# Branch gates, branch products and attention's queries and keys computed transposed, in a two-block mixer network on one core

## The chip, the cores and the metric

The kernel runs on 1 core of one Trainium2 chip. The metric is the device time of one execution in microseconds, as the median of several runs.

## The reference, cut to what matters

One sequence of 256 tokens, 1024 channels, float32. A first block of two layers (mixer, then a dense or an expert feed-forward part, then a gated side input) is followed by a second block of two layers with another mixer. The parts that the change touches are in the two mixers:

```
# first block's mixer, once per layer; u is the normalised input, (256, 1024)
rq, rk, rv, rg, gqkv, gz, ga, gb, mg_ret, mg_gdn = split(u @ w_in)
q = rotary(rq, pos); k = rotary(rk, pos)           # 4 heads of 128
# rotary: x1, x2 = halves of a head; [x1 * cos - x2 * sin, x2 * cos + x1 * sin]
y_ret = (norm(retention(q, k, rv)) * silu(rg)) @ w_br_ret
y_gdn = (norm(gated_delta_rule(gqkv ...)) * silu(gz)) @ w_br_gdn
merged = sigmoid(mg_ret) * y_ret + sigmoid(mg_gdn) * y_gdn
h = h + merged @ w_out

# second block's mixer, once per layer
uf, dq, dk, dv, gq, gk, gv, gr, glr = split(u @ w_in_2)
pool = windowed means of uf, mixed by a small matrix
diff = for each of 4 heads: (softmax(q1 k1') - lam * softmax(q2 k2')) @ dv    # q, k from dq, dk
gla  = gated linear attention of gq, gk, gv, with gate gr and decay from glr
h = h + concat(pool, diff, gla) @ w_out
```

## The kernel before

Everything lives in SBUF for the whole run except weights, which stream from HBM in tiles of 128 by 1024 values (`raw`). Matmuls run on tiles of the program's type fp32r. To keep accuracy, each product is made of three matmuls: every weight tile is split into a high part `whi` by ACT (L248) and a rest `wlo` by DVE (L249), every activation into `uh` and `ul` in the same way (L251 on ACT, L252 on DVE), and the three products high by high, low by high and high by low go into the same PSUM bank.

There are two forms of a product. `linear` (matmuls at L196 to L198) holds 128 tokens of the activation still and streams 512 columns of weights past them; its result is natural, tokens on partitions. `blocks_t` (L240 to L242) holds a 128 by 128 block of weights still and streams the 256 tokens past it; its result is transposed, channels on partitions, two blocks of 128 channels in one bank. `blocks_t` wants the weights in another order in HBM, which the host prepares. Whatever is computed in natural form and is wanted with channels on partitions goes through `split_t` (L264: a transpose on TensorE against the identity `c_ident`, into a `pt` bank, then L251 and L252).

The program keeps PSUM in two pools of four banks: `mm` for the products, `pt` for everything else.

In the first block's mixer the natural form made: the rotary queries and keys `qr`, `kr` (four wide DVE operations per 128 tokens, with one position per partition), the gates `mgr` and `mgg` (ACT, sigmoid with the token's norm `R` as a per-partition factor, L646), the two branch products (L743 and the line ahead of it multiply by the gate and add). Retention transposes each head of `qr` and `kr` (L702: 4 transposes a head, 16 a layer) and copies them out (`qkt`, L705) before its scores (L707, L708) and outputs (L713 to L715). The merged result `mgr` is transposed (L264, 16 a layer) for `w_out`.

In the second block's mixer `dq` and `dk` are made in natural form and copied out of PSUM by ACT with the factor `R` (L1055); after the gated linear attention (`gla`; its last matmuls are L1147 and L1149, its output `glo`, L1152 and L1153, then eight squares on ACT, L1157, a reciprocal root in 12 small DVE operations, L145 to L153, and eight products `gy`, L1165, transposed at L264) they are transposed a head at a time (L1189, 16 a layer) and copied to `qt` and `kz` (L1193 to L1196). `kz` keeps the two half-heads in separate zero-padded blocks. The scores are L1206.

The order on each engine is decided when the program is built, by a list scheduler with its own estimates: it starts instructions by priority, the chains (retention, delta rule, gla, softmax) ahead of projections, and projections fill TensorE's waits as far as weights and free PSUM banks allow. After that every engine has its list of instructions, in that order. A bank of `mm` can be filled again only after ACT or DVE has emptied it.

`row_of` (L295 to L300) turns the per-token factor `R` into a row `Rrow`, equal on all partitions, by two float32 matmuls (L297) and a DVE copy (L299). Before, the first block's mixer calls it once per layer, and the second block's mixer doesn't.

## Time and profile before

| | |
|---|---|
| median of 3 runs | 1987.58 us (1984.10 to 1988.67) |
| the profiled execution | 1985.24 us, its span 1983.5 us |
| TensorE busy | 1947.6 us, 98% of the span |
| VectorE busy | 1459.9 us, 74% |
| ScalarE busy | 1186.6 us, 60% |
| mean granted TensorE clock | 0.996 of full speed |

Times in rows are microseconds from the start of the span. Matmuls overlap in TensorE's pipeline, so a matmul's own duration says less than the distance from its start to the next one's start. A row that ends in `xN` is N instructions of one kind that follow each other; a bracket at a row's end is idle time of the engine just ahead of it, and what ended that.

### The profile page before, as it was taken

To read this page: it belongs to the slowest core of one execution; us is meant where nothing else is said; L and a number is where in the kernel's file an instruction comes from. 1 tells how busy PE (TensorE), PEld (TensorE's weight loads), DVE (VectorE), ACT (ScalarE), POOL (GpSimd) and SP (SyncE) were. 2 spreads that over 40 slices of the span, in tenths; PEclk is the share of its full clock that TensorE was granted. 3 is DMA by queue.
4 is the path that set the end of the run, shared out by engine and by line. 5 is a ranking of instruction groups with operands and counts; after the bars stand their busy time and mean duration, and the time that the engine had idled before them with its cause. 6 is when DMAs were issued, how large, how long until landed. Compare 5 with 4: busy or idle time off the path is not lost. (4 is left out here: it accounts for less than half of the span.)

```text
span 1983.5 us, 30564 instructions
## 1 busy us (share of the span) xinstructions
PE 1947.6 (98%) x11386; PEld 1665.2 (84%) x11386; DVE 1459.9 (74%) x2569; ACT 1186.6 (60%) x1885; POOL 14.3 (1%) x29
## 2 busy tenths in 40 slices
PE   7999999999999999999999999998999999999998
PEld 7888887999889878877888888786879898879896
DVE  7986756666479877666998888897877555776565
ACT  7862454544478743445877777776765454565453
POOL 0000000000000000001000000000000000000000
PEclk9999999999999999999999999999999999999999
DMA  9553445565565553456798989994735665635653
GB/s 241 150 169 113 133 161 175 179 186 187 191 176 157 157 156 105 151 193 217 253 350 300 354 298 355 325 355 159 227 107 159 191 184 179 182 96 176 189 188 106
DMA packets 244926, 393.27 MB, mean 198 GB/s; under 512 B 23297, under 2 KB 100001, under 8 KB 244769
## 3 DMA queue, kind: packets, MB, share of 16 engines
q1 hardware_dynamic: 235344, 389.14, 61.2%
q10 hardware_dynamic: 9424, 2.10, 0.5%
q8 instruction: 91, 1.49, 0.3%
q14 instruction: 67, 0.54, 0.1%
HBM read 389.35 MB, written 1.84 MB: 197 GB/s over the span
## 5 line engine op out<-in xcount | busy, mean ns | idle before, releaser
L249 DVE TENSOR_TENSOR wlo<-raw,whi 128x1024 fp32r<-128x1024 f32 (+3 forms) x748 | 878.8, 1184 | 380.6 <-ACT whi L248 373.1
L248 ACT ACTIVATE whi<-raw 128x1024 fp32r<-128x1024 f32 (+3 forms) x748 | 766.1, 1027 | 586.9 <-PE mm L198 354.5
L196 PE MATMUL mm<-whi,uh 128*128 128x512 f32 (+3 forms) x1312 | 504.8, 385 | 2.0 <-ACT uh L251 1.5
L197 PE MATMUL mm<-wlo,uh 128*128 128x512 f32 (+3 forms) x1312 | 504.0, 385 | 1.0 <-DVE wlo L249 0.5
L198 PE MATMUL mm<-whi,ul 128*128 128x512 f32 (+3 forms) x1312 | 503.5, 386 | 0.8 <-DVE ul L252 0.6
L197 PEld LDWEIGHTS mm<-wlo,uh 128*128 128x128 f32 x1312 | 247.0, 188 | 51.9 <-DVE wlo L249 6.9
L196 PEld LDWEIGHTS mm<-whi,uh 128*128 128x128 f32 x1312 | 247.1, 188 | 48.4 <-ACT uh L251 4.6
L198 PEld LDWEIGHTS mm<-whi,ul 128*128 128x128 f32 x1312 | 246.3, 188 | 46.2 <-DVE ul L252 2.2
L240 PE MATMUL mm<-uh,whi 128*128 128x256 f32 x864 | 242.3, 281 | 0.7 <-ACT uh L251 0.6
L242 PE MATMUL mm<-uh,wlo 128*128 128x256 f32 x864 | 242.0, 280 | 0.0
L241 PE MATMUL mm<-ul,whi 128*128 128x256 f32 x864 | 242.0, 280 | 0.0
L240 PEld LDWEIGHTS mm<-uh,whi 128*128 128x128 f32 x864 | 162.7, 188 | 1.8 <-ACT uh L251 1.1
L241 PEld LDWEIGHTS mm<-ul,whi 128*128 128x128 f32 x864 | 162.6, 188 | 0.2
L242 PEld LDWEIGHTS mm<-uh,wlo 128*128 128x128 f32 x864 | 162.7, 188 | 0.0
L198 PE MATMUL mm<-whi,hl 128*128 128x512 f32 x344 | 136.4, 397 | 0.0
L197 PE MATMUL mm<-wlo,hh 128*128 128x512 f32 x344 | 135.7, 394 | 0.0
L196 PE MATMUL mm<-whi,hh 128*128 128x512 f32 x344 | 134.5, 391 | 0.0
L224 PE MATMUL mm<-uh,wlo 128*128 128x256 f32 x384 | 109.9, 286 | 0.0
L222 PE MATMUL mm<-uh,whi 128*128 128x256 f32 x384 | 109.6, 285 | 0.0
L223 PE MATMUL mm<-ul,whi 128*128 128x256 f32 x384 | 109.6, 285 | 0.0
L251 ACT ACTIVATE uh<-pt,cols 128x256 fp32r<-128x256 f32 x152 | 65.1, 472 | 20.8 <-PE pt L264 7.4
L197 PEld LDWEIGHTS mm<-wlo,hh 128*128 128x128 f32 x344 | 64.6, 188 | 15.2
(419 smaller groups left out, 2423.1 us busy)
## 6 DMA issues: line engine op xcount, KB each, us to landing
raw<-in_w_in_dram SPq DMA_DIRECT2D x176, 512.0 KB, 3.7
raw<-in_w_mlp_dram SPq DMA_DIRECT2D x128, 512.0 KB, 3.7
raw<-in_exp_w_down_dram SPq DMA_DIRECT2D x80, 512.0 KB, 6.7
raw<-in_exp_w_gate_dram SPq DMA_DIRECT2D x64, 512.0 KB, 5.6
raw<-in_exp_w_up_dram SPq DMA_DIRECT2D x64, 512.0 KB, 6.1
raw<-in_w_out_dram SPq DMA_DIRECT2D x32, 512.0 KB, 3.6
raw<-in_exp_w_gate_dram SPq DMA_DIRECT2D x32, 384.0 KB, 4.6
raw<-in_exp_w_up_dram SPq DMA_DIRECT2D x32, 384.0 KB, 4.2
```

The source lines that it names most:

```text
L196: nc.tensor.matmul(o, uh[:, u0 + k, tk], hi, start=first and k == 0, stop=False)
L197: nc.tensor.matmul(o, uh[:, u0 + k, tk], lo, start=False, stop=False)
L198: nc.tensor.matmul(o, ul[:, u0 + k, tk], hi, start=False, stop=last and k == kt - 1)
L222: nc.tensor.matmul(o[:, m], hi[:, k], uh[:, k, :], start=k == 0, stop=False)
L223: nc.tensor.matmul(o[:, m], hi[:, k], ul[:, k, :], start=False, stop=False)
L224: nc.tensor.matmul(o[:, m], lo[:, k], uh[:, k, :], start=False, stop=k == 7)
L240: nc.tensor.matmul(o[:, i], hi[:, k], uh[:, k, :], start=k == 0, stop=False)
L241: nc.tensor.matmul(o[:, i], hi[:, k], ul[:, k, :], start=False, stop=False)
L242: nc.tensor.matmul(o[:, i], lo[:, k], uh[:, k, :], start=False, stop=k == 7)
L248: nc.scalar.activation(hi, src, AF.Copy)
L249: nc.vector.tensor_sub(lo, src, hi.bitcast(F32))
L251: nc.scalar.activation(hi, src, AF.Copy, scale=col)
```

## The change

All in the two mixers; the layout of six weights on the host goes with it.

- First block's mixer: rotary queries and keys come out of `blocks_t` (weights `w_rqk`, with the two halves of the heads on separate blocks), so that DVE makes two products with cosine and sine rows and four short sums and differences for each pair of blocks, and `qkt` is written directly in the form that the scores want. `cosR` and `sinR`, the rows with the token's factor in them, are made once a layer by POOL. Retention's 16 transposes and four copies a layer go.
- The gates `mgr`, `mgg` come out of `blocks_t` (`w_mg`): DVE multiplies by `Rrow`, ACT takes the sigmoid. The branch products come out of `blocks_t` too; the last of them is split for `w_out` right where it is merged, and the 16 transposes of `mgr` a layer go.
- Second block's mixer: `dq` and `dk` come out of `blocks_t` (`w_dqk`). DVE multiplies them by `Rrow` straight into `qt` and `kz`; the 16 transposes a layer and their copies go. `Rrow` is made here by a new call of `row_of`.

Counted in the two programs, 1152 matmuls of 128 by 512 become 2304 of 128 by 256; 96 transposes go, and 4 small float32 matmuls (two calls of `row_of`) are new. Bytes from HBM and the number of weight splits stay.

```diff
-            def rotary(name, dst):
-                o = [s.mm(), s.mm()]
-                s.linear(u, W, 0, 8, OFF[name], 512, o)
...
+            def rotary(n):
+                for pr in range(2):
+                    o = s.mm().rearrange("p (m t) -> p m t", t=T)
+                    s.blocks_t(u, a["w_rqk"][l], n * 4 + pr * 2, o)
+                    c, d = (gc.tile([P, 2, T], F32, name=x, bufs=1) for x in ("rcos", "rsin"))
+                    nc.vector.tensor_mul(c, o, cosR[:, None, :].to_broadcast([P, 2, T]))
+                    nc.vector.tensor_mul(d, o, sinR[:, None, :].to_broadcast([P, 2, T]))
+                    for i in range(2):
+                        r, r2 = (slice(x * 64, x * 64 + 64) for x in (i, 1 - i))
+                        nc.vector.tensor_sub(qkt[r, pr * 2 + i, n], c[r, 0], d[r, 1])
+                        nc.vector.tensor_add(qkt[r2, pr * 2 + i, n], c[r, 1], d[r, 0])
...
-                        nc.tensor.transpose(p[:, n * T + t * P:n * T + (t + 1) * P], x[:, t, hd * P:(hd + 1) * P],
-                                            s.ident)
-                qkt = g2.tile([P, 512], F32, name="qkt")
-                nc.scalar.activation(qkt, p, AF.Copy)
...
-            for d, n in ((mg2, "mgg"), (mg, "mgr")):
-                for c in (0, 512):
-                    gate_block(d, OFF[n], c, 512, AF.Sigmoid)
+            for d, i in ((mg2, 8), (mg, 0)):
+                for m in range(0, 8, 2):
+                    o = s.mm().rearrange("p (m t) -> p m t", t=T)
+                    s.blocks_t(u, wg, i + m, o)
+                    nc.vector.tensor_mul(d[:, m:m + 2], o, Rrow[:, None, :].to_broadcast([P, 2, T]))
+                    nc.scalar.activation(d[:, m:m + 2], d[:, m:m + 2], AF.Sigmoid)
...
+            out = (s.up.tile([P, 8, T], F32R, name="uh"), s.up.tile([P, 8, T], F32R, name="ul"))
+            for m in range(0, 8, 2):
+                o = s.mm().rearrange("p (m t) -> p m t", t=T)
+                s.blocks_t(yu, a["w_br_ret"][l], m, o)
+                x = mg[:, m:m + 2]
+                nc.vector.tensor_mul(x, x, o)
+                nc.vector.tensor_add(x, x, mg2[:, m:m + 2])
+                s.split(out[0][:, m:m + 2], out[1][:, m:m + 2], x)
+            yu = out
-            yu = s.split_t(mg, 8)
             s.residual(h, yu, a["w_out"][l], 8)
...
-            proj(256, 512, copy(dq))
-            proj(768, 512, copy(dk))
+            Rrow = s.row_of(R, g1.tile([P, T], F32, name="Rrow"))
+            qts = []
+            for pr in range(2):
+                o = s.mm().rearrange("p (m t) -> p m t", t=T)
+                s.blocks_t(u, a["w_dqk"][l], pr * 2, o)
+                qt = g2.tile([P, 2, T], F32, name="qt")
+                nc.vector.tensor_mul(qt, o, Rrow[:, None, :].to_broadcast([P, 2, T]))
+                qts += [qt[:, 0], qt[:, 1]]
+                o = s.mm().rearrange("p (m t) -> p m t", t=T)
+                s.blocks_t(u, a["w_dqk"][l], 4 + pr * 2, o)
+                for i in range(2):
+                    r = slice(i * 64, i * 64 + 64)
+                    nc.vector.tensor_mul(s.kz[r, pr * 2:pr * 2 + 2, i], o[r], Rrow[r, None, :].to_broadcast([64, 2, T]))
```

The order, at the three places that matter below. Rows read line, operation, output, inputs and size; lines of the changed kernel are 2 or 3 lower than those of the kernel before for the same code.

TensorE in the second block's mixer, from the last matmuls of gla (L1147, L1149) to the transposes of its output `gy`, before:

```order
L1147 MATMUL pt<-S_18612,qc 128x256
L1149 MATMUL pt<-gla,am 128x64
L196 MATMUL mm<-whi,uh 128x256
L197 MATMUL mm<-wlo,uh 128x256
L198 MATMUL mm<-whi,ul 128x256
...
L196 MATMUL mm<-whi,uh 128x512
L197 MATMUL mm<-wlo,uh 128x512
L198 MATMUL mm<-whi,ul 128x512
...
L264 MATMUL pt<-c_ident,gy 128x128
L1189 MATMUL pt<-c_ident,dq 128x128 x2
```

The same place in the changed kernel (L1144, L1146 are gla's last matmuls, L238 to L240 the last 12 matmuls of the keys by `blocks_t`, L295 the matmuls of `row_of`, L194 to L196 the projection `uf`):

```order
L1144 MATMUL pt<-S_19515,qc 128x256
L1146 MATMUL pt<-gla,am 128x64
L238 MATMUL mm<-uh,whi 128x256
L239 MATMUL mm<-ul,whi 128x256
L240 MATMUL mm<-uh,wlo 128x256
...
L262 MATMUL pt<-c_ident,gy 128x128
L295 MATMUL pt<-c_ident,R 128x128
L262 MATMUL pt<-c_ident,gy 128x128 x3
L295 MATMUL pt<-c_ident,R 128x128
L194 MATMUL mm<-whi,uh 128x256
```

Before, 39 matmuls of 256 columns (`uf`) and 14 of 512 (`dv`) stand between gla and `gy`; now 12 matmuls of 256 columns stand there, and `uf` and `dv` come behind the transposes and `row_of`.

VectorE at that place in the changed kernel, from gla's output to the products that empty the banks of queries and keys (L143 to L151 the reciprocal root, L297 the copy of `row_of`, L1173 and L1179 the products with `Rrow`):

```order
L1150 TENSOR_TENSOR glo<-glo,pt 128x512
L247 TENSOR_TENSOR wlo<-raw,whi 128x1024
L143 TENSOR_SCALAR rs_v_19551<-so 128x8
...
L151 SCALAR_TENSOR_TENSOR rs_y_19553<-rs_t_19556,rs_y_19553 128x8
L1162 SCALAR_TENSOR_TENSOR gy<-glo,rs_y_19553,gy 128x64 x8
L297 COPY Rrow<-pt 128x256
L250 SCALAR_TENSOR_TENSOR ul<-pt,cols,uh 128x256
L1173 TENSOR_TENSOR qt<-mm,Rrow 128x512
L250 SCALAR_TENSOR_TENSOR ul<-pt,cols,uh 128x256
L1179 TENSOR_TENSOR kz<-mm,Rrow 64x2x256 x2
```

The copy of `Rrow` stands behind gla's output, and the products that free the four banks stand behind it; one weight split (`wlo`) of those that stood inside the reciprocal root before is gone from there.

TensorE at the end of the first block's merge, from the last branch product to `w_out`, before:

```order
L198 MATMUL mm<-whi,ul 128x512
L264 MATMUL pt<-c_ident,mgr 128x128 x10
L196 MATMUL mm<-whi,uh 128x512
L197 MATMUL mm<-wlo,uh 128x512
L196 MATMUL mm<-whi,uh 128x512
L197 MATMUL mm<-wlo,uh 128x512
L264 MATMUL pt<-c_ident,mgr 128x128 x6
```

and in the changed kernel:

```order
L240 MATMUL mm<-uh,wlo 128x256
L194 MATMUL mm<-whi,uh 128x512
L195 MATMUL mm<-wlo,uh 128x512
L196 MATMUL mm<-whi,ul 128x512
```

The transposes of `mgr` are gone, and `w_out` follows the last branch product directly.

## Rows read from the trace of the kernel before

**Rows 1.** The page, engines' busy time; the costliest groups (busy, mean ns, idle before)
```profile
PE 1947.6 (98%) x11386; PEld 1665.2 (84%) x11386; DVE 1459.9 (74%) x2569; ACT 1186.6 (60%) x1885; POOL 14.3 (1%) x29
...
L240 PEld LDWEIGHTS mm<-uh,whi 128*128 128x128 f32 x864 | 162.7, 188 | 1.8 <-ACT uh L251 1.1
```

**Rows 2.** Windows of linear alone, then blocks_t alone: us, PE busy (instructions), granted clock
```profile
251.00:281.00 30.00, 30.00 (x130) 1.00 0.57 178
...
368.00:408.00 40.00, 40.00 (x343) 1.00 0.55 172
```

**Rows 3.** Timeline of TensorE at the end of the merge: start, us, instruction
```profile
331.87 1.03 PE L264 MATMUL pt<-c_ident,mgr 128*128 128x128 f32 x8
...
335.17 0.88 PE L264 MATMUL pt<-c_ident,mgr 128*128 128x128 f32 x6 [0.31 <-DVE mgr L743]
335.80 0.72 PE L198 MATMUL mm<-whi,ul 128*128 128x512 f32 x2
```

**Rows 4.** Timeline of TensorE at one of retention's eight visits
```profile
227.76 0.38 PE L702 MATMUL pt<-c_ident,qr 128*128 128x128 f32 x2
...
228.11 0.48 PE L196 MATMUL mm<-whi,uh 128*128 128x512 f32 x1
228.43 0.39 PE L197 MATMUL mm<-wlo,uh 128*128 128x512 f32 x1
```

**Rows 5.** Timelines of PE, ACT, DVE where a branch's input is split
```profile
284.71 0.50 PE L196 MATMUL mm<-whi,uh 128*128 128x512 f32 x1 [0.34 <-ACT uh L251]
...
284.19 2.66 ACT L251 ACTIVATE uh<-pt,cols 128x256 fp32r<-128x256 f32 x7
...
284.89 2.92 DVE L252 SCALAR_TENSOR_TENSOR ul<-pt,cols,uh 128x256 fp32r<-128x256 f32 x7
```

**Rows 6.** Timeline of TensorE in the second block's mixer, from gla to the scores
```profile
1446.89 0.33 PE L1149 MATMUL pt<-gla,am 128*128 128x64 f32 x2
1447.03 0.36 PE L196 MATMUL mm<-whi,uh 128*128 128x256 f32 x1
...
1455.30 0.33 PE L264 MATMUL pt<-c_ident,gy 128*128 128x128 f32 x1
...
1459.40 1.03 PE L1206 MATMUL pt<-kz,qt 128*128 128x256 f32 x3
```

**Rows 7.** Timelines of ACT and DVE over gla's output, same stretch
```profile
1447.09 0.60 ACT L1152 ACTIVATE glo<-pt 128x512 f32<-128x512 f32 x1 [5.15 <-PE pt L1147]
...
1451.46 0.17 DVE L145 TENSOR_SCALAR rs_v<-so 128x8 f32<-128x8 f32 x1
...
1453.14 0.17 DVE L151 TENSOR_TENSOR rs_t<-rs_y 128x8 f32<-128x8 f32 x1
1453.23 1.22 DVE L249 TENSOR_TENSOR wlo<-raw,whi 128x1024 fp32r<-128x1024 f32 x1
1454.37 0.16 DVE L152 TENSOR_TENSOR rs_t<-rs_t,rs_v 128x8 f32<-128x8 f32 x1
...
1454.77 1.46 DVE L1165 SCALAR_TENSOR_TENSOR gy<-glo,rs_y,gy 128x64 f32<-128x64 f32 x7
```

**Rows 8.** Rows of tile Rrow (ns min/median/max), and one split on DVE
```profile
L769 DVE TENSOR_TENSOR sl<-mm,Rrow x11: 691/692/694, 371.5 to 484.1; 128x512 f32<-128x512 f32 x11
L299 DVE COPY Rrow<-pt x3: 416/416/425, 24.3 to 589.5; 128x256 f32<-128x256 f32 x3
...
1458.48 0.48 DVE L252 SCALAR_TENSOR_TENSOR ul<-pt,cols,uh 128x256 fp32r<-128x256 f32 x1
```

**Rows 9.** After TensorE's longest wait inside the run: timeline row, then windows with granted clock
```profile
1366.52 3.65 PE L264 MATMUL pt<-c_ident,h 128*128 128x128 f32 x16 [3.94 <-DVEq L861]
...
1364.00:1366.00 2.00, 0.00 (x0) 0.50 0.03 8
...
1368.00:1370.00 2.00, 2.00 (x12) 0.50 0.80 263
1370.00:1372.00 2.00, 1.95 (x8) 0.94 0.91 265
```

More of the change, by code (lines that the diff above doesn't have):

```diff
@@ L48, in _consts @@
     cos, sin = np.cos(ang).astype(f), np.sin(ang).astype(f)
-    cd = np.concatenate([cos, cos], 1).reshape(2, P, P).transpose(1, 0, 2)
-    sd = np.concatenate([-sin, sin], 1).reshape(2, P, P).transpose(1, 0, 2)
-    out["cos"] = cd.reshape(P, 256)
-    out["sin"] = sd.reshape(P, 256)
+    out["cos"] = np.concatenate([cos, cos], 1).T
+    out["sin"] = np.concatenate([sin, sin], 1).T
     lg = np.log1p(-np.exp2(-5.0 - np.arange(4)))
@@ L362, in mixer1 @@
             u, R = s.norm_t(h, s.col("norm_mix", l))
-            Rrow = s.row_of(R, g1.tile([P, T], F32, name="Rrow"))
+            Rrow = s.row_of(R, m8.tile([P, T], F32, name="Rrow"))
             gz = m8.tile([P, 2, D], F32, name="gz")
             sg = m8.tile([P, 2, D], F32, name="sg")
-            qr, kr = (m8.tile([P, 2, 512], F32, name=n) for n in ("qr", "kr"))
+            qkt = m8.tile([P, 4, 2, T], F32, name="qkt")
             V = s.up.tile([P, 2, D], F32, name="uh")
@@ L677, in mixer1 @@
                 gc = e2.enter_context(s.tc.tile_pool(name="gc", bufs=2))
+                cosR, sinR = (gc.tile([P, T], F32, name=n, bufs=1) for n in ("cosR", "sinR"))
+                nc.gpsimd.tensor_mul(cosR, s.c["cos"], Rrow)
+                nc.gpsimd.tensor_mul(sinR, s.c["sin"], Rrow)
                 small_blocks()
@@ L691, in mixer1 @@
                     else:
-                        rotary(f, qr if f == "rq" else kr)
+                        rotary("qk".index(f[1]))
         with ExitStack() as es:
@@ L696, in mixer1 @@
             tab = {"ret": s.cst("ret", g1)}
-            mg, mg2 = (g1.tile([P, 2, D], F32, name=n) for n in ("mgr", "mgg"))
+            mg, mg2 = (g1.tile([P, 8, T], F32, name=n) for n in ("mgr", "mgg"))
             for hd in range(4):
-                p = s.pb()
-                for n, x in enumerate((qr, kr)):
-                    for t in range(2):
-                        nc.tensor.transpose(p[:, n * T + t * P:n * T + (t + 1) * P], x[:, t, hd * P:(hd + 1) * P],
-                                            s.ident)
-                qkt = g2.tile([P, 512], F32, name="qkt")
-                nc.scalar.activation(qkt, p, AF.Copy)
                 ps = s.pb()
-                nc.tensor.matmul(ps[:, :T], qkt[:, T:T + P], qkt[:, :T], start=True, stop=True)
-                nc.tensor.matmul(ps[:, T:T + P], qkt[:, T + P:], qkt[:, P:T], start=True, stop=True)
+                q, k = qkt[:, hd, 0], qkt[:, hd, 1]
+                nc.tensor.matmul(ps[:, :T], k[:, :P], q, start=True, stop=True)
+                nc.tensor.matmul(ps[:, T:T + P], k[:, P:], q[:, P:], start=True, stop=True)
                 st = g2.tile([P, 384], F32, name="st")
@@ L1181, in mixer2 @@
             lam = ls[:, 3:4]
[L1182 removed]
             sd = g1.tile([P, 8], F32, name="sd")
[L1184 to L1196 removed]
+            scs, mxs, ats = [], [], []
             for hd in range(4):
@@ L1205, in mixer2 @@
                     pv = ps[:, :2 * n].rearrange("p (m j) -> p m j", m=2)
-                    nc.tensor.matmul(ps[:, :2 * n], qts[hd][:, t * P:(t + 1) * P], s.kz[hd][:, :, :n],
+                    nc.tensor.matmul(ps[:, :2 * n], qts[hd][:, t * P:(t + 1) * P], s.kz[:, hd, :, :n],
                                      start=True, stop=True)
@@ L1352, in run @@
             s.c = {n: s.cst(n, cp) for n in C2}
-            s.kz = []
-            for i in range(4):
-                kz = cp.tile([P, 2, T], F32, name=f"kz{i}")
-                nc.gpsimd.memset(kz, 0.0)
-                s.kz.append(kz)
+            s.kz = cp.tile([P, 4, 2, T], F32, name="kz")
+            nc.gpsimd.memset(s.kz, 0.0)
             for l in range(2):
@@ L1376, in _arrays, with blocks @@
         out[k] = n[k][0]
-    for k in ("w_mlp1_2", "ffn_w_gate", "ffn_w_up"):
-        w = out[k].reshape(-1, 8, P, out[k].shape[-1] // P, P).transpose(0, 3, 2, 1, 4)
-        out[k] = w.reshape((2,) * (k == "w_mlp1_2") + (-1, P, D))
+    def blocks(w):
+        w = w.reshape(-1, 8, P, w.shape[-1] // P, P).transpose(0, 3, 2, 1, 4)
+        return w.reshape(-1, w.shape[1], P, D)
+    for k in ("w_mlp1_2", "w_br_gdn", "w_br_ret"):
+        out[k] = blocks(out[k])
+    for k in ("ffn_w_gate", "ffn_w_up"):
+        out[k] = blocks(out[k])[0]
+    out["w_mg"] = blocks(n["w_in"][:, :, OFF["mgr"]:])
+    out["w_dqk"] = blocks(n["w_in_2"][:, :, 256:1280])
+    rqk = n["w_in"][:, :, :1024].reshape(2, D, 2, 2, 2, 2, 64).transpose(0, 1, 2, 3, 5, 4, 6)
+    out["w_rqk"] = blocks(rqk.reshape(2, D, 1024))
     cols, rows = [], []
```

46 lines of the change are left out of this document (6 added, 40 removed).

## The prediction

> **What bounds the kernel now.** I read the page's busy times first: TensorE is busy 1947.6 of 1983.5 us, VectorE 74%, ScalarE 60% [rows 1]. So a microsecond counts where TensorE has more or less to do, or must wait. Then I read the windows for the spacing of the two forms of product, the timelines of the places that the change touches, and last the order of the changed program, for what now stands behind what. A matmul's cost is the distance to the next start; durations overlap.
>
> **The change part by part.** *Width.* 1152 matmuls of 512 columns become 2304 of 256. 130 wide ones fill 30 us, 343 narrow ones fill 40 us [rows 2]: .2308 and .1166 us each, so a pair of narrow ones costs .0024 more than a wide one. Over 1152 pairs that is 2.8 us. The counts are good to one or two instructions (and the profile can miss records), which moves it between -1 and +7; I take +3.
>
> The Trainium skill ("TensorE: Matmul & The Clock Gate", Back-to-back issue gap) gives sustained 131 ns at 512 columns and 81 ns at 128, because the load of the still operand shares the spacing; a straight line between them puts 256 columns at an estimated 98 ns, and the 1152 pairs would then cost 75 us more. The windows here say otherwise: .2308 and .1166 us, nearly in proportion to columns.
>
> *End of the merge.* From the first transpose of `mgr` at 331.87 to the first matmul behind them at 335.80 pass 3.93 us [rows 3], in which four matmuls of `w_out` run (4 x .2308 = .92). The other 3.0 us are the 16 transposes and waits for the merged halves. Now `w_out` follows directly; its first k-steps need earlier pairs only, and the last pair's product, sum and two splits (about 2.8 us if each takes the .691 of [rows 8]) have 36 wide matmuls (8.3 us) as cover. If that cover failed, up to 2 us would come back. The second layer has the same order: -6.0.
>
> *Retention.* One visit of four transposes takes .35 us to the next product, and that product's successor starts .32 us later instead of .23 [rows 4]: .44 us with the switch. Eight visits: -3.5. The ACT copies behind them are off the path, since other products fill those waits. The rotary work on DVE (two products of .691 [rows 8] and four short sums for each pair of blocks, some 1.5 us a layer more than before by my count) and two POOL products lie beside projections, which fill TensorE there before and now: 0, within 3 either way.
>
> *Splits of a branch's input.* After the 16 transposes of `gz` (`sg`) the wide form needs one `uh`, `ul` for six matmuls, 1.4 us; `blocks_t` needs one for three narrow ones, .35 us. ACT makes one `uh` in 2.66/7 = .38 us, DVE one `ul` in 2.92/7 = .42 [rows 5]. Eight at DVE's pace are .56 us longer than eight at .35, and a weight split in between adds up to 1.2. Four such places, .6 each: +2.4, between 0 and 6.
>
> *Second mixer, per layer.* Here the order decides. Before, 39 narrow and 14 wide matmuls stand between gla's last matmul and the transposes of `gy`; they run from 1447.03 to 1455.30 [rows 6] and cover the whole chain that makes `gy`. They could run because ACT had emptied the banks of `dq`, `dk`. Now only 12 narrow ones stand there (1.4 us, to 1448.45): queries and keys keep all four `mm` banks until DVE multiplies them by `Rrow`, and `row_of` stands among the transposes of `gy`. So `uf` and `dv` can't start. The chain by its rows: `glo` leaves PSUM at 1447.09, the root's first step is at 1451.46, and its last ends by 1454.77 [rows 7]; in the new DVE order the weight split inside it is gone (the step after it starts at 1454.37, 1.23 after its forerunner at 1453.14, where others stand .2 apart), so the root ends near 1453.74. The eight `gy` at 1.46/7 = .21 each follow: the first transpose can start near 1454.1, the last near 1455.5. Then `row_of` to 1455.7, the copy `Rrow` .416, an `ul` .48, the first product .691 [rows 8]: the first `uf` starts near 1457.3. From 1448.45 to 1457.3 are 8.85 us; .44 of it are the transposes of `gy`, .44 the new matmuls, 8.0 idle.
>
> Against that: from 1447.03 to the scores at 1459.40 [rows 6] the old kernel has 12.37 us with 39 narrow and 20 wide matmuls (9.2), 4 transposes of `gy` and 16 of `dq`, `dk` (.105 each as six take .63 from 335.17 on [rows 3]: 2.1), so 1.1 are waits and switches that go. The 16 transposes save 1.7. Net 8.0 + .4 - 1.1 - 1.7 = +5.6. The displaced `uf` and `dv` must still run, behind it. Could they fill waits there? In the scores and the softmax TensorE is hardly ever idle now, because `dv` fills them already; I give 0 to 2 us.
>
> *The clock.* After the one long wait inside the run (3.94 us) the granted clock is .50, that is 1.2 GHz, and returns to .94 in the window 1370 to 1372, some 3.6 us after work resumed at 1366.52 [rows 9]. Half speed over 3.6 us costs 1.8. The new wait of 5.7 us ahead of the first `gy` is longer, so the same is likely: +1.8 per layer, between 0 and 3.6. Two layers: 2 x (5.6 + 1.8) = +14.8, between +7 and +22.
>
> *Sum:* 3 - 6 - 3.5 + 2.4 + 14.8 = +10.7 us. On the profiled execution (1985.24) that gives 1995.9. The median of the runs is 2.3 above it, and the forecast is for a median: **1998**.
>
> **The rivals.** *The gain arrives and the wait doesn't hurt* (faster): `uf` and `dv`, pushed behind, fill waits of the scores and softmax chains, so the 8.0 us come back there, and the clock stays. For it: two chains overlap there, and DVE is the slower engine. Against it: the old trace shows TensorE filled there. Sum 10.7 - 2 x (8.0 - 1.1 + 1.8) = -6.7: 1981.
>
> *The wait is there, the clock holds, part is made up:* transposes interrupt the wait and one us a layer comes back: 10.7 - 2 x 1.8 - 2 x 1 = +5.1: 1993. It decides if the granted clock stays at 1.00 in the second mixer.
>
> *The clock falls and stays low* (far slower): behind the wait come short float32 matmuls and waits for softmax, and 1.2 GHz lasts 10 us a layer, not 3.6: +3.2 a layer, with splits at their bound (+6): 10.7 + 6.4 + 3.6 = +20.7: 2008.
>
> *Narrow matmuls are paced by the weight load:* a load lasts 188 ns [rows 1]; if it set the spacing, 1152 x (2 x .188 - .2308) = +167 us, 2155. The windows of 343 narrow ones exclude it for long stretches. The skill's page named above has this rule, with less. Chance 1%.
>
> *It doesn't do what it says*: the program shows the transposes gone; under 1%.
>
> **How the numbers follow.** A median can be told from no change here beyond about 0.2%, 4 us: faster below 1983.6, slower above 1991.6. The forecast has a chance of .45 (1994 to 2004, all slower); the partly made-up wait .21 (half within 0.2%, half slower); the gain that arrives .20 (.17 faster, .03 same); the long low clock .13; the weight load .01. So faster .17, same .14, slower .69. For 8 in 10 I leave out the lower half of the gain's case and the upper end of the low clock's: 1981 to 2008.
>
> **What would show it.** In the new profile: PE waiting about 5.7 us for `gy` (L1162 on DVE) and then about 1.5 for `qt` (L1173), in both layers, with the granted clock below 1 there; no transposes and no wait between `w_out` and the last branch product; windows with 343 narrow matmuls in 40 us in the gates. Wrong would be: no such wait; a clock of 1.00 through the second mixer; new waits of TensorE for `uh` or `ul` of more than 1 us at each branch; or a second block that does not start about 5 us earlier (2 of the 3 for width, as 768 of the 1152 pairs are in the first; - 6 - 3.5 + 2.4).

## The result, and the profile after

The changed kernel takes **2020.63 us** (median of 4 runs, 2019.87 to 2020.89), the kernel before in the same session 1986.26 (1984.10 to 1988.67): a ratio of **1.0173, 95% interval 1.0161 to 1.0185**, or 34.4 us more. The direction was forecast; the size (10.7 us) was not, and the time lies above the range.

The page, engines' busy times, and the mean granted clock, of the changed kernel:

```profile
PE 1963.0 (97%) x12450; PEld 1732.4 (86%) x12450; DVE 1485.6 (74%) x2607; ACT 1171.7 (58%) x1853; POOL 18.8 (1%) x30
...
core 0: 2018.8 us, clock 0.987
```

Against [rows 1], TensorE has 1064 more matmuls in its record and is busy 15 us longer in a span that is 35 us longer. Of the whole, the mean clock holds the first hint: .987 of full speed over 2018.8 us is 26 us of lost full-speed time, .996 over 1983.5 was 8. Up to 18 of the 34 us can therefore be clock, where the prediction had allowed 3.6. It is an upper bound, since a low clock costs nothing while TensorE waits. Counting only TensorE's busy time (in windows of 2 us, each weighted by what its granted clock lacks to 1), the low clock cost 19.4 us in the changed kernel's profile and 3.6 in the old one's, an estimate of 15.8 more.

The view of waits of TensorE (who waited for whom: us in total, times, longest), the changed kernel:

```profile
PE pt L262 <- DVE gy L1162: 11.2, 2, 5.6
...
PE mm L194 <- DVE qt L1173: 3.0, 2, 1.5
PE mm L240 <- DVE wlo L247: 2.3, 2, 1.1
PE mm L239 <- DVE ul L250: 2.3, 6, 0.7
PE pt L508 <- ACT cs L410: 2.2, 2, 1.2
PE pt L706 <- DVE st L703: 1.2, 2, 0.7
...
PE mm L238 <- ACT uh L249: 1.0, 4, 0.3
```

The same view of the kernel before has these in their place:

```profile
PE pt L264 <- DVE mgr L743: 1.9, 4, 0.6
PE mm L196 <- ACT uh L251: 1.5, 4, 0.5
PE pt L536 <- DVE Tn L526: 1.5, 2, 0.8
```

The lines with `gy` and `qt` are the second mixer's wait, twice 5.6 and twice 1.5 us, as forecast to a tenth. `wlo`, `cs` and `st` are new waits of .6 to 1.2 us in places of the first mixer that the change was not thought to touch: they belong to the delta rule's stretch and to the head of retention. `ul` and `uh` belong to the inputs of the branches. All lines of the view add up to 44.9 us in the changed kernel and to 25.1 in the old one.

The distances between the same matmuls in both kernels, read from the two timelines, say where the 35 us of span lie. The marks are `Rrow`, retention's first output (L713, after the change L706), the first transpose of `h` behind the merge, and the first transpose of `glr` in the second block:

| stretch of TensorE | before, us | after, us | difference |
|---|---|---|---|
| start to `Rrow` of the first layer | 22.9 | 24.7 | +1.8 |
| first layer: projections and delta rule, to retention's first output | 209.0 | 215.4 | +6.5 |
| first layer: retention, gates, branches, merge | 116.0 | 119.0 | +3.1 |
| rest of the first layer | 240.2 | 239.4 | -0.9 |
| second layer: projections and delta rule | 208.1 | 210.1 | +2.0 |
| second layer: retention to merge | 116.4 | 117.1 | +0.6 |
| rest of the first block, to `glr` | 502.5 | 506.9 | +4.4 |
| second block's mixer, first layer | 83.2 | 91.8 | +8.6 |
| second block's mixer, second layer | 84.3 | 93.6 | +9.3 |
| everything else | 401.0 | 400.8 | -0.2 |

The first block was forecast to start the second block 5 us earlier. It does so 17.6 us later. Not all of that belongs to the change: the first row reads 22.9 to 25.3 and the rest of the first block 500.9 to 507.8 in the profiles of the experiments below, whatever the edit.

The timeline of TensorE in the second block's mixer of the changed kernel (start, us, instruction; the bracket is the wait ahead of it), against [rows 6]:

```profile
1464.67 0.28 PE L240 MATMUL mm<-uh,wlo 128*128 128x256 f32 x1
1470.53 0.47 PE L262 MATMUL pt<-c_ident,gy 128*128 128x128 f32 x1 [5.57 <-DVE gy L1162]
1470.79 0.63 PE L295 MATMUL pt<-c_ident,R 128*128 128x128 f32 x2
...
1474.15 0.58 PE L194 MATMUL mm<-whi,uh 128*128 128x256 f32 x1 [1.51 <-DVE qt L1173]
```

And the windows of the same stretch (us, length, busy time of TensorE with its instructions, granted clock, DMA share, GB/s):

```profile
1464.00:1468.00 4.00, 0.96 (x9) 0.93 0.01 2
1468.00:1472.00 4.00, 1.47 (x6) 0.50 0.43 131
1472.00:1476.00 4.00, 2.49 (x12) 0.50 0.00 0
1476.00:1480.00 4.00, 4.00 (x18) 0.79 0.00 0
1480.00:1484.00 4.00, 4.00 (x31) 1.00 0.00 0
```

The clock goes to .50 (1.2 GHz) within the wait and is back only in the window that ends at 1480, some 7 us after work resumed at 1470.53. From [rows 9] it had been put at 3.6. By the estimate above, 2.8 us of work were lost here and 4.1 in the second layer, 6.9 where 3.6 had been forecast.

The clock falls in the first mixer too, with no long wait next to it. The windows of the delta rule's last part in the first layer, changed kernel, and then the kernel before at the same place:

```profile
192.00:200.00 8.00, 8.00 (x103) 0.85 0.01 2
200.00:208.00 8.00, 8.00 (x58) 0.50 0.19 69
208.00:216.00 8.00, 8.00 (x39) 0.79 0.00 2
```

```profile
192.00:200.00 8.00, 8.00 (x102) 1.00 0.23 68
200.00:208.00 8.00, 8.00 (x56) 1.00 0.22 67
208.00:216.00 8.00, 8.00 (x54) 1.00 0.45 133
```

The counts of the first two windows are alike, but the work is not. From 192 to 208 the old kernel runs 33 product matmuls of 512 columns between the delta rule's short ones, the changed kernel 6 of 256 columns and 4 of 512. The low stretch begins near 197.5, among the delta rule's matmuls on blocks of 32 by 32, and costs 6.8 us, about the 6.5 of the table's second row.

The end of the merge, against [rows 3]:

```profile
343.38 0.28 PE L240 MATMUL mm<-uh,wlo 128*128 128x256 f32 x1
343.50 0.40 PE L194 MATMUL mm<-whi,uh 128*128 128x512 f32 x1
```

There are no transposes and no wait between the last branch product and `w_out`, as the change says.

### The profile page after: what moved, and what is told of

It is laid out like the page before. It is cut to its first block, busy times and chain, and to the rows that moved or that the text cites. A ratio compares the mean times of both kernels' runs of the same rounds, so it can differ in the third digit from the quotient of the medians.

```text
span 2018.8 us, 32702 instructions
## 1 busy us (share of the span) xinstructions
PE 1963.0 (97%) x12450; PEld 1732.4 (86%) x12450; DVE 1485.6 (74%) x2607; ACT 1171.7 (58%) x1853; POOL 18.8 (1%) x30
## 5 line engine op out<-in xcount | busy, mean ns | idle before, releaser
L239 PE MATMUL mm<-ul,whi 128*128 128x256 f32 x1632 | 459.6, 282 | 2.3 <-DVE ul L250 2.3
L240 PE MATMUL mm<-uh,wlo 128*128 128x256 f32 x1632 | 458.3, 281 | 2.3 <-DVE wlo L247 2.3
L238 PE MATMUL mm<-uh,whi 128*128 128x256 f32 x1632 | 458.7, 282 | 1.1 <-ACT uh L249 1.0
L194 PE MATMUL mm<-whi,uh 128*128 128x512 f32 (+3 forms) x928 | 354.5, 384 | 4.9 <-DVE qt L1173 3.0
L195 PE MATMUL mm<-wlo,uh 128*128 128x512 f32 (+3 forms) x928 | 353.8, 382 | 0.6 <-DVE wlo L247 0.2
L196 PE MATMUL mm<-whi,ul 128*128 128x512 f32 (+3 forms) x928 | 351.8, 380 | 0.6 <-DVE ul L250 0.6
L239 PEld LDWEIGHTS mm<-ul,whi 128*128 128x128 f32 x1632 | 307.4, 188 | 4.6 <-DVE ul L250 4.0
L238 PEld LDWEIGHTS mm<-uh,whi 128*128 128x128 f32 x1632 | 306.8, 188 | 3.5 <-ACT uh L249 2.1
L240 PEld LDWEIGHTS mm<-uh,wlo 128*128 128x128 f32 x1632 | 307.4, 188 | 2.8 <-DVE wlo L247 2.7
L194 PEld LDWEIGHTS mm<-whi,uh 128*128 128x128 f32 x928 | 177.7, 192 | 36.9 <-DVE qt L1173 3.6
L195 PEld LDWEIGHTS mm<-wlo,uh 128*128 128x128 f32 x928 | 177.7, 192 | 34.5 <-DVE wlo L247 5.1
L196 PEld LDWEIGHTS mm<-whi,ul 128*128 128x128 f32 x928 | 177.6, 191 | 28.5 <-DVE ul L250 1.0
L196 PE MATMUL mm<-whi,hl 128*128 128x512 f32 x344 | 136.4, 397 | 0.0
L194 PE MATMUL mm<-whi,hh 128*128 128x512 f32 x344 | 134.4, 391 | 0.0
L222 PE MATMUL mm<-uh,wlo 128*128 128x256 f32 x384 | 109.8, 286 | 0.0
L220 PE MATMUL mm<-uh,whi 128*128 128x256 f32 x384 | 109.7, 286 | 0.0
L221 PE MATMUL mm<-ul,whi 128*128 128x256 f32 x384 | 109.6, 285 | 0.0
L250 DVE SCALAR_TENSOR_TENSOR ul<-pt,cols,uh 128x256 fp32r<-128x256 f32 x152 | 66.8, 478 | 14.8 <-ACT uh L249 13.8
```

The costliest lines, as they stand in the source:

```text
L194: nc.tensor.matmul(o, uh[:, u0 + k, tk], hi, start=first and k == 0, stop=False)
L195: nc.tensor.matmul(o, uh[:, u0 + k, tk], lo, start=False, stop=False)
L196: nc.tensor.matmul(o, ul[:, u0 + k, tk], hi, start=False, stop=last and k == kt - 1)
L220: nc.tensor.matmul(o[:, m], hi[:, k], uh[:, k, :], start=k == 0, stop=False)
L221: nc.tensor.matmul(o[:, m], hi[:, k], ul[:, k, :], start=False, stop=False)
L222: nc.tensor.matmul(o[:, m], lo[:, k], uh[:, k, :], start=False, stop=k == 7)
```

## The experiments

They are in four groups. Each takes the kernel before or the changed kernel and one edit; "before" is always the kernel before in the same session (1986.7 to 1987.2 us). Theory at the start: the second mixer's order loses the most, the rest is in the delta rule's stretch. A difference in us is one of medians; a ratio comes with its 95% interval and is not formed from the medians, so the two can differ by some us.

### The second mixer's order

**m2_only**: of the change only the last part, `dq` and `dk` transposed; first block as before.

> The kernel before with the second mixer's part of the change alone. Order theory: the second mixer alone costs 16 to 19 us, so about 2004. Width rival (the loss goes by the number of narrow pairs, 192 of 1152): a sixth of the 34 us, so about 1992.

Measured 2004.78 us (2004.45 to 2009.02), ratio 1.0096 [1.0078, 1.0115]: +18.0. Its waits are those of the whole change, word for word in size:

```profile
PE pt L264 <- DVE gy L1164: 11.2, 2, 5.6
...
PE mm L196 <- DVE qt L1175: 3.0, 2, 1.5
```

Its clock is .991 in the mean of the runs, against .996 before: up to 9.8 of the 18 us.

**m2_early**: the same, with `row_of` called as soon as the last projection ahead of gla is issued, so that `Rrow` is there when the banks of queries and keys are full (the edit against m2_only):

```diff
             proj(1792, 512, copy(gla))
+            Rrow = s.row_of(R, g1.tile([P, T], F32, name="Rrow"))
...
-            Rrow = s.row_of(R, g1.tile([P, T], F32, name="Rrow"))
             qts = []
```

> The kernel before with the second mixer's part alone, and in it the row Rrow made right behind the first two projections. Order theory: of the 18 us that this part costs with the late row nothing is left; 16 fewer transposes a layer (1.7 us) against .45 of row_of and about .5 of width give 0 to 2 us less than before, 1984 to 1987. Rival (the part is slow for another reason, its DVE products or its narrow matmuls): 1990 or more. The first mixer is that of the kernel before, so the granted clock should stay near .996 in all executions if the first mixer's part is what lowers it.

Measured 1986.05 us (1984.40 to 1989.08), ratio .9993 [.9982, 1.0003], clock .996. The 18 us are gone with one moved line. No gain is shown, although 32 transposes and their copies are gone (about 3.4 us of TensorE at .105 each); the interval reaches from 3.6 us faster to .6 slower, so the 0 to 2 us that were expected are not excluded. In its waits neither `gy` nor `qt` appears.

**row_early**: the whole change with this line moved.

> The changed kernel with one edit: in the second block's mixer the row Rrow is made right behind the first two projections, not behind gla. Order theory (queries and keys hold all four product banks until Rrow exists, so TensorE waits for gla's output): the wait of 5.6 us for gy and the 1.5 us for qt go in both layers, the granted clock stays at 1 there, and the time falls by 16 to 20 us from 2020.6, to about 2002. Width rival (narrow matmuls themselves are dearer than the windows say): nothing of this changes their number, so the time stays within 3 us of 2020.

Measured 1997.80 us (1990.82 to 2003.86), ratio 1.0053 [1.0031, 1.0075]: 22.8 us less than the changed kernel, a little more than the 16 to 20 that were expected. Its runs spread over 13 us, so the upper figure is loose. TensorE in the second mixer is filled again, the granted clock is 1.00 from 1440 to 1480, and the scores start between the transposes of `gy`:

```profile
1471.16 0.28 PE L196 MATMUL mm<-whi,ul 128*128 128x256 f32 x1
1471.28 0.39 PE L194 MATMUL mm<-whi,uh 128*128 128x512 f32 x1
...
1475.01 0.39 PE L195 MATMUL mm<-wlo,uh 128*128 128x512 f32 x1
1475.51 0.33 PE L262 MATMUL pt<-c_ident,gy 128*128 128x128 f32 x1
1475.68 1.89 PE L1201 MATMUL pt<-kz,qt 128*128 128x256 f32 x6
```

So the order, the one call of `row_of` that stood behind gla, is shown to be the cause of 18 to 23 us of the 34.

### The first mixer's two parts

**rot_only**: the rotary part alone. **br_only**: gates and branch products alone.

> The kernel before with the rotary queries and keys of the first mixer alone. Delta-stage theory (the new rotary work on VectorE and the moved loads delay the delta rule's chain, about 4 us a layer, and in the first layer the clock falls for another 4): 8 to 13 us slower than before, about 1996. Width rival: 192 of 1152 pairs, a sixth of 34 us, about 1992, with no clock loss between 190 and 215 us. My prediction's term for this part was a gain of 3.5 us: 1983.

> The kernel before with the gates and the branch products of the first mixer alone. By the trace's division (excess at the splits, less the transposes of mgr, plus 768 narrow pairs at .0035): between 3 us faster and 2 us slower, about 1986. Width rival: 768 of 1152 pairs, two thirds of 34 us, about 2009.

Measured: rot_only 1991.53 us (1988.69 to 1996.62), ratio 1.0023 [1.0013, 1.0034]: +4.8. br_only 1997.78 (1990.92 to 2000.57), ratio 1.0044 [1.0028, 1.0060]: +11.0, where between a gain of 3 and a loss of 2 was expected. 18.0 + 4.8 + 11.0 = 33.8; by the ratios the parts are 19.1, 4.6 and 8.7, together 32.4, and with the repeat below in place of 11.0 they are 30.0. So the parts add up to the whole within a few us. The expectation for br_only is missed by both theories that stood there. For rot_only the time is the width rival's (1992), but that rival put all 34 us down to width; the waits for `wlo` (2.3 us) and `cs` (2.7) of the other theory are in its profile, and so is a low clock, in the second layer (from 762 on) and not in the first.

**br_again**: the same kernel as br_only in another session, for a second profile.

> The kernel with gates and branch products transposed in both layers once more, for a second profile and more executions. If its loss is its own: +9 to +13 us again, with the same waits in the profile in the router's stretch, ahead of the branch inputs and in the delta rule. If the first profile's waits in the delta rule were one execution's, they are gone here while the time stays.

Measured 1994.30 us (1990.29 to 2002.87), ratio 1.0043 [1.0026, 1.0061]: +7.2, less than the 9 to 13 that were expected. The loss is the kernel's own; the two sessions put it at 11.0 and 7.2 by medians, at 1.0044 and 1.0043 by ratios. **b_l0** and **b_l1** do the edit in the first or in the second layer only.

> Gates and branch products transposed in the first layer only; the second layer keeps the natural form (as in the kernel before). The whole edit in both layers cost 11 us. Theory 'each layer costs the same': +4 to +7 us (1990 to 1994). Theory 'the loss sits in one layer, behind changed orders there': either about 0 to +2 or +9 to +11; the sum of this run and of its twin for the second layer is 11 in either case. Theory 'the loss isn't of the place but of a program that runs at a lower clock': the granted clock is at .994 to .995 here as well, and the time as much longer.

> The twin: gates and branch products transposed in the second layer only. Same in each layer: +4 to +7 us. In one layer: 0 to +2 or +9 to +11. Together with the run for the first layer: 11 us.

Measured: b_l0 1990.36 us (1985.02 to 1994.31), ratio 1.0018 [1.0006, 1.0030], +3.3; b_l1 1990.83 (1987.52 to 1993.84), 1.0021 [1.0012, 1.0031], +3.8. Together 7.1, the 7.2 of br_again: the loss is not in one layer's order, the edit of each layer costs about half of it.

**width_b**: the natural form of the kernel before with all its transposes, only that 704 of the 768 wide matmuls in gates and branch products are cut into two halves.

```diff
+            ops = ((uh, hi), (uh, lo), (ul, hi))
+            for n, (x, wt) in enumerate(ops):
+                a0, z = first and k == 0 and n == 0, last and k == kt - 1 and n == 2
+                for c in ((slice(0, cn // 2), slice(cn // 2, cn)) if half and not (a0 or z) else (slice(0, cn),)):
+                    nc.tensor.matmul(o[:, c], x[:, u0 + k, tk], wt[:, c], start=a0, stop=z)
```

> The kernel before, natural form and all its transposes kept, but 704 of the 768 wide matmuls of the gates and branch products are each cut into two of 256 columns with the same operands. Width alone by the spacings of the windows (.2308 wide, .1166 to .118 narrow): +1.7 to +3.6 us. Theory 'the narrow form itself lets the clock fall or waits on loads': +8 us or more and a granted clock of .994 or .995. If it is within +4, width isn't the cause of the 11 us.

Measured 1994.20 us (1992.60 to 1995.73), ratio 1.0038 [1.0025, 1.0051]: +7.1, with the clock at .997 in four runs of five, as high as before. So a cut costs 7.1/704 = .010 us a pair here, not .0024 (which would have been 1.7), and it does so without the clock: the halfway result that neither theory had. A cut is not only width: each half loads its still operand again (PEld x12090 against x11386, as many as matmuls). The profile agrees. From the first transposes of `gz` to those of `sg`, kernel before, width_b, br_again:

```profile
282.46 1.91 PE L264 MATMUL pt<-c_ident,gz 128*128 128x128 f32 x16
307.28 1.91 PE L264 MATMUL pt<-c_ident,sg 128*128 128x128 f32 x16
```

```profile
284.67 1.03 PE L266 MATMUL pt<-c_ident,gz 128*128 128x128 f32 x8
310.03 1.91 PE L266 MATMUL pt<-c_ident,sg 128*128 128x128 f32 x16
```

```profile
283.76 1.91 PE L264 MATMUL pt<-c_ident,gz 128*128 128x128 f32 x16
309.55 1.91 PE L264 MATMUL pt<-c_ident,sg 128*128 128x128 f32 x16
```

That is 24.82, 25.36 and 25.79 us for the same 96 wide matmuls' worth. The stretch ahead of it, from retention's first output to `gz`, with nearly all of the gates' matmuls in it, takes 50.64, 52.70 and 51.91 us in these kernels, and in the second layer 50.62, 52.70 and 51.91: the same loss in both layers. In the form of the change it is 1.3 us a layer for the 181 pairs there, .007 each. No transposes have gone from these three kernels up to there, and TensorE shows no wait in the stretch. In width_b this is the cut alone; in br_again it is the other form with all that belongs to it.

### The delta rule's stretch and the clock

**base_wait**: the kernel before, with a chain of small DVE operations in the delta rule lengthened by about a microsecond a layer (four more sign changes that cancel); forms and order as before.

```diff
-                nc.vector.tensor_scalar(na, na, -1.0, None, op0=OP.mult)
+                for _ in range(5):
+                    nc.vector.tensor_scalar(na, na, -1.0, None, op0=OP.mult)
```

> The kernel before with the sign flip at the head of the delta rule's small triangular blocks done five times and not once (the same result), some 1.2 us more on that chain in each layer, all of the first mixer in its natural form. Theory (a longer wait of TensorE in the delta stage is enough for the clock to fall there): 3 to 10 us slower than before, a mean clock of .995 or less in most executions, a low stretch in the profile between 150 and 215 or 720 and 785 us. Rival (the narrow matmuls of the changed form let it fall): at most 2.4 us slower, clock .996 as before.

Measured 1990.66 us (1985.92 to 1992.93), ratio 1.0013 [1.0000, 1.0025]: +4.0. Its wait, in the profiled execution:

```profile
PE pt L537 <- DVE Tn L527: 3.3, 2, 1.7
```

This is 1.8 us more than before (1.5), and 1.8 is half of the loss. By the ratio the loss is anything between 0 and 5.0 us, so the rival's "at most 2.4" is not excluded. The mean clock of the runs is .9951 against .9962, which can be the other 2.2. The profiled execution itself (1987.41 us, clock .996) has no low clock in the delta rule, so the link between the longer wait and the clock is seen in the runs' means and not in a trace: supported, not shown.

**rot_pool**: rot_only with the four short sums of a pair on GpSimd, to take 1.7 us of DVE's time from in front of the weight splits.

```diff
-                        nc.vector.tensor_sub(qkt[r, pr * 2 + i, n], c[r, 0], d[r, 1])
-                        nc.vector.tensor_add(qkt[r2, pr * 2 + i, n], c[r, 1], d[r, 0])
+                        nc.gpsimd.tensor_sub(qkt[r, pr * 2 + i, n], c[r, 0], d[r, 1])
+                        nc.gpsimd.tensor_add(qkt[r2, pr * 2 + i, n], c[r, 1], d[r, 0])
```

> Rotary part alone (as rot_only, 1991.5), with its four short sums per pair on GpSimd and not on VectorE. If VectorE's 3.1 us per pair are what delays the weight split and the delta rule's masks, 2 to 4 us less than rot_only, about 1988; if the loss is the late load of the small blocks or the clock, within 1 us of 1991.5; if GpSimd is so slow that retention waits for it, slower.

Measured 2005.11 us (2003.36 to 2006.00), ratio 1.0083 [1.0062, 1.0105]: worse by 13.6 than rot_only. One sum on DVE in the changed kernel, two here on GpSimd, and then two rows of DVE here, the second beside the second sum:

```profile
155.84 0.42 DVE L658 TENSOR_TENSOR qkt<-rcos,rsin 64x256 f32<-64x256 f32 x1
```

```profile
156.46 1.66 POOL L658 TENSOR_TENSOR qkt<-rcos,rsin 64x256 f32<-64x256 f32 x1 [36.55 <-DVE rsin L654]
...
747.08 1.61 POOL L659 TENSOR_TENSOR qkt<-rcos,rsin 64x256 f32<-64x256 f32 x1
```

```profile
162.15 1.33 DVE L524 TENSOR_TENSOR Tn<-tc,c_mask 128x1024 f32<-128x1024 f32 x1 [1.14 <-DMA tc<-dt]
...
746.41 1.69 DVE L247 TENSOR_TENSOR wlo<-raw,whi 128x1024 fp32r<-128x1024 f32 x1 [0.21 <-ACT whi L246]
```

The 32 sums take .74 us in the median on GpSimd, and those that run beside a weight split up to 1.74. The split is longer too: 1.69 us instead of the usual 1.2. So the edit takes less from DVE than was planned. TensorE's waits for `Tn` are 5.0 us in both layers together instead of 1.5, and the clock is .990. The row of L524 shows what makes `Tn` late (DVE starts on it at 162.15, in rot_only at 160.61): DVE waits for a transfer, `tc` from `dt`, and not for GpSimd. Why that transfer ends later here is not shown.

**all_fix** (the whole change, early `Rrow`, sums on GpSimd), **rot_first** and **rot_last** (row_early with the rotary blocks first or last in the list that orders the fillers of the delta rule, that is the projections that run in its waits), **no_br** (rot_first without gates and branches):

> The changed kernel with the early row and the rotary sums on GpSimd. Order theory with VectorE's load: some 3 us below row_early, about 1995, still slower than before because the first mixer's clock falls; a gain on before would need the clock to hold: 1981 to 1984 then (96 transposes of .109 less 1152 pairs at .004 less row_of .9: 5 us of work fewer).

> row_early with the rotary queries and keys asked for ahead of the delta rule's groups in the list of fillers (their matmuls then run before its solve, and matmuls of 512 columns fill the solve and the state steps as in the kernel before). Filler theory (the clock falls in the state steps because only 17 matmuls of 256 columns stand there where 17 of 512 stood): no low stretch of 13.7 us there in the profile, a clock of .995 or more in most executions, 1990 to 1995. Rival (the clock falls for the first mixer's other narrow matmuls, or by chance whatever fills it): as row_early, 1991 to 2004 with a median near 1998.

> row_early with the values' projection asked for ahead of the rotary part: matmuls of 512 columns fill the solve and the first half of the state steps, narrow rotary ones the second half. Filler theory: the low stretch goes or is shorter, 1990 to 1997; retention's start may wait for the last rotary sums, 1 to 3 us. Rival: as row_early, median near 1998.

> Rotary part (asked for early, as in rot_first) and second mixer's part (row made early), with the gates and branch products of the kernel before. If the parts add up and the clock holds: the 32 transposes of retention and 32 of the second mixer (7.0 us) less 384 pairs at .004 (1.5) less row_of (.9) less the wait for the small blocks' load and the switch (2 to 4): 1983 to 1987. If the rotary part costs as it did alone, 1991.

Measured:

| kernel | us (lowest to highest) | ratio, 95% interval | mean clock |
|---|---|---|---|
| all_fix | 2010.16 (1998.81 to 2014.27) | 1.0091 [1.0061, 1.0121] | .990 |
| rot_first | 2004.13 (1998.72 to 2010.79) | 1.0076 [1.0050, 1.0102] | .992 |
| rot_last | 1994.66 (1989.33 to 2006.01) | 1.0044 [1.0027, 1.0061] | .994 |
| no_br | 1992.45 (1986.63 to 2000.38) | 1.0025 [1.0012, 1.0037] | .995 |

None comes down to the kernel before. rot_first puts wide matmuls back as fillers of the last part of the delta rule: 10 of 512 columns stand among the 32 by 32 matmuls, as many as in the kernel before, where the changed kernel has 6 of 256. In its second layer the clock falls there all the same (752 to 768), so narrow fillers are not needed for the fall. rot_last came out within the 1990 to 1997 of that idea, but its clock falls there too (744 to 756).

What the slowest share is a longer wait for `Tn` (4.6 us in two layers for rot_first, 4.1 for all_fix, 5.0 for rot_pool, against 1.5 before), and a lower clock with it. But the changed kernel and row_early wait .8 us for `Tn`, and their profiled executions ran at .987 and .992, so this wait alone does not set the clock or the time. In several traces the clock does fall right behind it, as in all_fix (windows, then the wait):

```profile
160.00:162.00 2.00, 0.00 (x0) 1.00 0.86 311
162.00:164.00 2.00, 1.82 (x9) 0.53 0.58 223
```

```profile
162.18 3.65 PE L534 MATMUL pt<-Tn,A 128*128 128x64 f32 x16 [2.50 <-DVE Tn L524]
```

The same holds behind 2.54 us in rot_pool and 3.34 in rot_last. It does not hold behind the 1.69 and 1.64 us of base_wait and the 2.1 of b_l0, where the clock stays at 1.00.

The long low stretch that begins among the 32 by 32 matmuls has no wait of TensorE right ahead of it. All 8 profiles of kernels with the rotary part have it, for 10 to 14 us at half speed, in one layer or (all_fix) in both; none of the 9 profiles without that part has it. The changed kernel has it in the first layer and row_early in the second, although the two differ by one line of the second block. So it goes with the rotary part, and in which layer it comes is not set by the order there.

No kernel of the four groups is faster than the kernel before; m2_early equals it.

## Why the prediction was right in sign and wrong in size

The measured 34.4 us are 23.7 more than the forecast 10.7. By an estimate from the two profiles, the 35.3 us of span are made up of TensorE's waits (+19.8), the low clock (+15.8), 1152 pairs at .007 (+8.1, see below) and two calls of `row_of` (+.9), less 96 transposes at .105 (-10.1): 34.5. The prediction had the second mixer's waits and the transposes about right. Short are the clock (3.6, now 15.8), the waits beside the rotary work (0, now 5.7) and the width (3, now 8.1): 23.0 of the missing 23.7. So three steps failed: the clock was asked only behind the second mixer's wait and put at nothing everywhere else, DVE's rotary work was put at 0, and the width was mis-sized.

**Second mixer, +14.8: right.** The order was read rightly, the two waits came as worked out (5.6 and 1.5 us), and alone it costs 18.0. Mis-sized is the clock inside this term: 3.6 us at half speed after a wait were taken from [rows 9], 7 were seen. By the estimate above, that costs 6.9 us in the two layers of the changed kernel and 5.3 in the profile of m2_only instead of 3.6, which is most or all of the 3.2 that the term lacks.

**Width, +3: too small.** The spacing was read from two undisturbed windows of [rows 2]. In a stage, with short matmuls and transposes in between, a pair costs .007 more than a wide matmul (1.3 us for 181 pairs), in width_b .010. Over 1152 pairs that is 8 to 12 us instead of 3. (The split of the pairs was wrong as well: 960 of the 1152 are in the first block, not 768.) The bound that the text gave (-1 to +7) was for miscounting in the window, and missed what a stream that is cut into pieces costs. The Trainium skill ("TensorE: Matmul & The Clock Gate", Back-to-back issue gap) would have it at .065 a pair by the estimate of the prediction; width_b's .010 disagrees with that size, while the sign is the page's.

**End of the merge, -6: nearly right.** In the first layer, from the first transpose of `mgr` (after the change, from the first matmul of `w_out`) to the transposes of `h` behind it pass 15.92 us with 55 wide matmuls before and 15.64 with 65 after; at .232 each, 3.2 us beyond the matmuls became .6. That is -2.6 where -3.0 a layer was forecast.

**Splits, +2.4: nearly right.** The waits for `ul` and `uh` (2.3 and 1.0 us, over ten times) stand for the 1.5 of before; from `gz` to `sg` the changed kernel takes 1.2 us more in the first layer and 1.0 in the second, width included.

**Retention, -3.5, and the rotary work beside projections, "0, within 3 either way": the second is a step that failed.** The transposes are gone from the visits as read. But rot_only costs 4.8 us where -3.5 and some width were forecast. In the first layer of the changed kernel the rotary products and sums stand on DVE in front of three weight splits, and TensorE waits for one of these:

```profile
154.51 0.69 DVE L653 TENSOR_TENSOR rcos<-mm,cosR 128x512 f32<-128x512 f32 x1 [3.45 <-PE mm L240]
...
157.59 3.50 DVE L247 TENSOR_TENSOR wlo<-raw,whi 128x1024 fp32r<-128x1024 f32 x3
```

```profile
158.87 0.39 PE L240 MATMUL mm<-uh,wlo 128*128 128x256 f32 x1 [1.14 <-DVE wlo L247]
```

3.1 us of DVE work (two products, four sums) hold the splits up, and TensorE's queue has nothing else in front. Two more waits come from transfers that DVE waits for, and TensorE behind it:

```profile
133.18 0.29 DVE L482 TENSOR_SCALAR X<-X 128x256 f32<-128x256 f32 x1 [1.61 <-DMA X<-da]
...
239.49 0.56 DVE L703 TENSOR_TENSOR st<-pt,c_ret 128x384 f32<-128x384 f32 x1 [1.97 <-DMA c_ret<-in_c_ret_dram]
```

They show up in TensorE's waits as `cs` (1.0 us here) and `st` (.7). With both layers `wlo`, `cs` and `st` make 2.3 + 2.2 + 1.2 = 5.7 us, most of what the forecast of the rotary part lacks. They are read from the trace; no run takes them away one by one. That projections "fill TensorE there before and now" was true of the count of matmuls, and false of what their operands wait for.

**Gates and branches together: forecast -1.8 by these terms, measured +7 to +11.** Width is some 3.5 of the difference (.007 instead of .0024 for 768 pairs). The merge came .8 short. What is left, about 4 to 8 us, lies outside the stretches that the edit rewrites. By the marks of the table, br_again's span is 9.0 us longer than that of the kernel before. Of this, +1.1 are in the first layer from retention to the next layer's `Rrow` and +.6 in the second from retention to the merge's end. Ahead of that, +3.7 are in the second layer's projections and delta rule, where TensorE waits 2.8 us for `Tn` (.7 before) and the low clock costs 1.7, and +3.4 in the rest of the first block, of which 2.3 are clock by the same estimate. (width_b has +5.2 and +3.2 in the first two places and 1.0 or less elsewhere.) Why wait and clock change in stretches that were not edited stays open; the transfer that `Tn` waits for took 2.6 to 6.1 us from issue to landing in these traces.

**The clock as a whole** is the largest miss (3.6 forecast, 15.8 by the estimate). The prediction asked what one wait does to it. The kernel before has two short stretches below full speed in its profile (936 to 944, and behind the wait of [rows 9]); the changed kernel has these two and three more, one in each layer of the second mixer and the one shown from 196 on in the first layer's delta rule. (A last one, behind TensorE's last work, costs nothing.) It is not settled what lets it fall in the delta rule: TensorE reads as busy 8.00 of 8.00 us in those windows. The Trainium skill ("TensorE: Matmul & The Clock Gate", A second HAM failure mode: psum-queue depth-cycling) tells of a kernel in which short idle times between groups of matmuls made the clock go up and down. The waits for `Tn` are of that kind: behind 2.50 us in all_fix and 3.34 in rot_last the clock falls, behind 1.69 in base_wait it does not. Ahead of the fall from 197.5 on in the changed kernel the trace shows no idle time, so for the costliest stretch (6.8 us) the cause stays open. In the 17 profiles it comes only with the rotary part; by what in that part is not shown.

**The rivals.** "The clock falls and stays low" was the nearest (2008); it had the right mechanism, in the second mixer, but not the first block's share. "The gain arrives" fell: `uf` and `dv` did not fill waits later. m2_early suggests besides that even without the wait there is little gain from the 32 transposes (3.4 us), since the added width takes part of it: 192 pairs at .007 to .010 are 1.3 to 1.9 us, beside .9 for two calls of `row_of`.

## What to carry to other kernels

Look up, for each bank of PSUM that a change makes wait for a new operand, where that operand is made in the engine's list: here one call placed 100 lines earlier was worth 18 to 23 us, more than every transpose the change removed. Before halving a matmul's width to save transposes, price the pair in the stage itself, with what interrupts it, not in an undisturbed stream. And work put "beside" a full TensorE on DVE is not free if DVE also makes TensorE's operands: ask what stands behind it in that list.

## What the runs showed that had not been expected

- Cutting 704 matmuls of 512 columns in two, with nothing else changed, cost 7.1 us (.010 us each) at an unchanged clock.
- A sum of 64 by 256 values took .74 us on GpSimd in the median of 32 where DVE took .42, and 1.66 while DVE was working on weight splits beside it; a split beside it took 1.69 where 1.2 is usual.
- The granted clock is not fixed by the program: executions of rot_only ran at .992 to .997 and took 1996.6 to 1988.7 us, those of row_early at .992 to .997 and 2003.9 to 1990.8.
- After the second mixer's wait the clock was back some 7 us after work resumed, and after the wait of [rows 9] 3.6 us after; the resumed work was sparser in the first case (2.49 us busy of 4.00 in the window 1472 to 1476).
- A low clock of 10 to 14 us that begins among the delta rule's 32 by 32 matmuls, with TensorE busy throughout: in all 8 profiles with the rotary part, in none of 9 without.
